# A hybrid decoder layer: the low half of the output stage's transposed operand moves from TensorE to a DMA transpose

## The chip, the cores and the metric

The kernel runs on one core of a Trainium2 chip. Its engines are TensorE (PE in the profile; PEld is its weight load), VectorE (DVE), ScalarE (ACT), GpSimd (POOL) and SyncE (SP), which issues the DMAs of this kernel. The metric is the device time of one execution in microseconds; less is better. A run's time is that of the whole execution, a profile's span reaches from the first to the last instruction.

## The reference

A decoder layer over 4096 positions of width 1024. Three groups of heads read one normalised input projection: a chunked gated MLP, a dilated attention in three dilations, and an attention into 256 memory tokens. Every branch is multiplied by its gate, the branches are laid side by side, and an output projection and the input are added:

```python
y = jnp.concatenate([y_g, y_a, y_m], axis=-1) @ w_out[l]
x = x + y
```

The change touches only this last product: `y` (4096 x 1024) times `w_out` (1024 x 1024), plus `x`.

## The kernel before

The kernel goes over the 32 tiles of 128 positions in several passes. Passes A and B project queries, keys, values and a gate, with the attention woven in; pass C (`pass_c`) does the memory attention and the gated MLP, and at its end begins the output stage. In between, results lie in DRAM: the three attention outputs (`o_d`), the gate (`ag_d`), the two other branches (`y_d`).

The output stage works tile by tile. `prep_y(n)` loads what it needs (tile `fo`, three parts, L742 and L743; `fsg`, L745; `fy`, L747 and L748; `fx`, the rows of x, L750), adds the three dilations (L751, L752), divides and gates (L754 to L759), finds each row's largest value (L762 to L765), and splits the scaled row into two f16 numbers: the high half on ACT (L767), the low half, what is left, on DVE (L768). Both are halves of one tile `hl` (name `fhl`), which has one buffer. TensorE transposes each half in eight 128x128 blocks into PSUM (L773, tile `fpt`), and ACT copies the result into `yT` (L774, name `fyT`, two buffers). `fo` and `fy` have two buffers each, `fsg` one.

The loop at the end calls `prep_y(n + 2)` and then does the product of tile n: `proj` (L222) multiplies high with high, high with low, and low with high, eight blocks each, so 24 matmuls of 512 columns and twice 24 of 256 columns, 72 in all (tile `fps`). `fin` scales and adds x (L977, L978), and the result is stored (L989).

The order of the instructions on each engine is not written out. A planner fixes it when the kernel is built, from modelled costs, with the order of the program as priority; at run time every engine and SP's queue of DMAs work strictly in that order. In the order that it found, the transposes of tile n + 2 stand between the 512-wide and the 256-wide matmuls of tile n.

Two earlier passes use a DMA transpose too: `qk_out` turns an `hl` tile of the same shape, 128 x 1024 in f16, into half of `stg` (L309), which ACT then copies (L312).

Of the kernel before, what the change touches and what calls it, by code (L numbers as in the profile page):

```python
# [9 lines left out]
F16 = mybir.dt.float16  # L10
# [8 lines left out]
P = 128  # L19
# [3 lines left out]
KT = D // P  # L23
# [11 lines left out]
def bcast(ap, n):  # L35
    s = list(ap.shape)
    return ap.unsqueeze(len(s)).broadcast_to(s + [n])
# [6 lines left out]
def shuffled(ap):  # L44

    return ap.rearrange("(j r) d -> r j d", r=R16)
# [25 lines left out]
def tile_hybrid_layer(ctx, tc, x, mem, norm_gain, w_in, gv_gain, wsT, gb, aqg, akg,  # L72
                      mem_gain, w_kv, mqg, mkg, w_out, out):
    nc = tc.nc
    V, S, G, TE, Q = nc.vector, nc.scalar, nc.gpsimd, nc.tensor, nc.sync
# [6 lines left out]
    def ps_tile(tag, shape, dt, name):  # L82
        return pp.tile(shape, dt, tag="po" if tag == "tr" else tag, name=name)
# [17 lines left out]
    idh = cp.tile([P, P], F16, name="idh")  # L101
# [249 lines left out]
    with tc.tile_pool(name="pA", bufs=2) as pA:  # L351
# [46 lines left out]
        for n in range(NT):  # L398
# [57 lines left out]
            if n == 12:  # L456
                wM, scM = got("wM")
                for j in range(2):
# [5 lines left out]
                    hl = pm.tile([P, 8, 2, HD], F16, name=f"mhl{j}", tag="hl", bufs=2)  # L464
# [274 lines left out]
    def prep_y(n):  # L739
        ot = pools[0].tile([P, 3, NH, 65], F32, name=f"fo{n}", tag="fo")  # L740
        for ci in range(2):
            Q.dma_start(ot[:, ci], o_d[ci][n * P:(n + 1) * P])  # L742
        Q.dma_start(ot[:, 2], o_d[2].rearrange("(r n j) h c -> n r j (h c)", r=R16, j=8)[n])  # L743
        sg = pools[0].tile([P, 512], F32, name=f"fsg{n}", tag="fsg", bufs=1)
        Q.dma_start(sg, shuffled(ag_d[n]))  # L745
        y = pools[0].tile([P, D], F32, name=f"fy{n}", tag="fy")
        Q.dma_start(y[:, 0:256], shuffled(y_d[n][:, 0:256]))  # L747
        Q.dma_start(y[:, 768:1024], shuffled(y_d[n][:, 256:512]))  # L748
        xr = pools[0].tile([P, D], F32, name=f"fx{n}", tag="fx", bufs=3)
        Q.dma_start(xr, shuffled(x[n * P:(n + 1) * P, :]))  # L750
        V.tensor_add(ot[:, 0], ot[:, 0], ot[:, 1])  # L751
        V.tensor_add(ot[:, 0], ot[:, 0], ot[:, 2])  # L752
        rd = pools[0].tile([P, NH], F32, name=f"frd{n}", tag="frd")
        V.reciprocal(rd, ot[:, 0, :, 64])  # L754
        yv = y[:, 256:768].rearrange("p (h c) -> p h c", c=HD)
        V.tensor_tensor(yv, ot[:, 0, :, 0:64], bcast(rd, HD), ALU.mult)
        for i in range(2):
            ys = y[:, 256 + i * 256:512 + i * 256]
            V.scalar_tensor_tensor(ys, ys, fag[:, i:i + 1], sg[:, i * 256:(i + 1) * 256],  # L759
                                   ALU.mult, ALU.mult)  # L760
        a = pools[0].tile([P, 8], F32, name=f"fa{n}", tag="fa", bufs=4)
        V.tensor_reduce(a[:, 0:1], y, AX.X, ALU.max, apply_absolute_value=True)  # L762
        V.tensor_scalar_max(a[:, 0:1], a[:, 0:1], 1e-30)
        V.reciprocal(a[:, 1:2], a[:, 0:1])
        V.tensor_scalar_mul(a[:, 1:2], a[:, 1:2], 2.0 ** 14)  # L765
        hl = pools[0].tile([P, 2, D], F16, name=f"fhl{n}", tag="fhl", bufs=1)
        S.activation(hl[:, 0, :], y, AF.Copy, scale=a[:, 1:2])  # L767
        V.scalar_tensor_tensor(hl[:, 1, :], y, a[:, 1:2], hl[:, 0, :], ALU.mult, ALU.subtract)  # L768
        yT = pools[0].tile([P, 2, KT, P], F16, name=f"fyT{n}", tag="fyT", bufs=2)
        for c in range(2):  # L770
            pt = ps_tile("po", [P, KT, P], F16, f"fpt{n}_{c}")
            for k in range(KT):
                TE.transpose(pt[:, k, :], hl[:, c, k * P:(k + 1) * P], idh)  # L773
            S.copy(yT[:, c], pt)  # L774
        yTs[n] = (yT, a, xr)

    pools, pool_cm = [], []
# [92 lines left out]
    def pass_c():  # L870
        xTs = {}
        for n in range(NT + LAG):
# [87 lines left out]
            if n == NT - 1 + SHIFT2:  # L960
                prep_y(0)
                prep_y(1)
# [7 lines left out]
    for n in range(NT):  # L970
        if n + 2 < NT:
            prep_y(n + 2)
        yT, a, xr = yTs.pop(n)
        res = pm.tile([P, D], F32, name=f"fr{n}", tag="stg", bufs=2)

        def fin(ps, c0, c, sc, k):
            V.tensor_scalar(a[:, k:k + 1], a[:, 0:1], sc[:, 0:1], 2.0 ** -28, ALU.mult, ALU.mult)  # L977
            V.scalar_tensor_tensor(res[:, c:c + 256], ps[:, c0:c0 + 256], a[:, k:k + 1],  # L978
                                   xr[:, c:c + 256], ALU.mult, ALU.add)

        ps = ps_tile("pj", [P, 512], F32, f"fps{n}_0")
        proj(ps, yT, wO0, 512)
        fin(ps, 0, 0, scO0[0], 2)
        fin(ps, 256, 256, scO0[1], 3)
        for i, (w, sc) in enumerate(ready["wO1"]):
            ps = ps_tile(("ps", "pa")[i], [P, 512], F32, f"fps{n}_{i + 1}")
            proj(ps, yT, w, 256)
            fin(ps, 0, 512 + 256 * i, sc, 4 + i)
        Q.dma_start(shuffled(out[n * P:(n + 1) * P, :]), res)  # L989
# [37 lines left out]
```

## Time and profile before

| | |
|---|---|
| time, median of three runs | 2130.55 us (2123.88 to 2132.16) |
| the profiled execution's own time | 2122.38 us |
| its span, first to last instruction | 2120.7 us |
| mean granted TensorE clock | 0.982 of 2.4 GHz |
| TensorE matmul busy | 1999.8 us, 94% |
| VectorE busy | 1467.6 us, 69% |
| ScalarE busy | 1204.4 us, 57% |
| GpSimd busy | 685.2 us, 32% |
| DMA, mean | 161 GB/s |
| output stage, first transpose to end | 1727.8 to 2120.7 us |

Busy shares are means over the whole span, and each stage has another limit; the output stage is the last 393 us of it. In the rows further down, an instruction has its start and its length in us, its engine, its line, what it writes and reads, and in brackets the engine's idle time before it with what ended that.

### The profile page before, as it was taken

The numbers are of one execution on the slowest core, as the hardware profiler recorded it, in microseconds if no ns is written. First come the engines' busy times: TensorE is split into PE (matmuls) and PEld (weight loads), VectorE is DVE, ScalarE is ACT, GpSimd is POOL, SyncE is SP. The second block draws the span as 40 slices with busy tenths as digits, with TensorE's granted clock in tenths as the row PEclk, the third lists the DMA queues.
The fourth block names the chain that finished last, engine by engine and source line by source line (L and its number), as shares of the span: only waits on it lengthen the run. The fifth ranks groups of instructions, "written<-read, shape, count | busy, mean of one in ns | idle before, by whom it ended". The sixth has DMA issues, their size and how long they took to land.

```text
span 2120.7 us, 45749 instructions
## 1 busy us (share of the span) xinstructions
PE 1999.8 (94%) x17025; PEld 1291.9 (61%) x17025; DVE 1467.6 (69%) x4332; ACT 1204.4 (57%) x2048; POOL 685.2 (32%) x632
## 2 busy tenths in 40 slices
PE   5999999988999998998999998999999989999999
PEld 4444444434466565665776766767757766767766
DVE  7665465466578686687787877868766676767762
ACT  6676676444478586684675765756757732222221
POOL 1212212121056264453554653535635620000000
PEclk9999999999999999999999999999999999999999
DMA  6777687585557868666447365474453367767662
GB/s 219 200 201 202 178 197 181 139 228 142 161 129 170 221 139 202 162 169 160 114 94 186 87 155 147 92 185 98 92 137 86 81 175 194 219 209 218 204 189 70
DMA packets 468959, 341.00 MB, mean 161 GB/s; under 512 B 294400, under 2 KB 404096, under 8 KB 466944
## 3 DMA queue, kind: packets, MB, share of 16 engines
q1 hardware_dynamic: 468736, 338.08, 62.1%
q8 instruction: 133, 2.18, 0.4%
q14 instruction: 90, 0.74, 0.1%
HBM read 198.52 MB, written 113.84 MB: 147 GB/s over the span
## 4 chain that ended last, share of the span: by engine, by line
PE 52%; DMA 6%; DVE 6%; issue 3%; ACT 3%; SPq 1%; POOL 1%; ACTq 0%; DVEq 0%; POOLq 0%
PE fps L222 15%; PE pc L222 13%; PE pag L222 4%; PE pqb L222 3%; PE s L588 3%; PE s L590 3%; PE pa L491 2%; PE o L615 1%; PE o L613 1%; PE o L611 1%; PE fpt L773 1%; DMA qn<-qnd 1%; DVE e L593 1%; DVE jk L498 1%; DMA qm<-q2t 1%
## 5 line engine op out<-in xcount | busy, mean ns | idle before, releaser
L545 POOL TENSOR_TENSOR pl<-e,ph 128x512 f16<-128x512 f32 (+1 forms) x384 | 412.0, 1085 | 342.3 <-ACT ph L544 246.9
L222 PE MATMUL pc<-wC,xTc 128*128 128x512 f16 (+1 forms) x2304 | 473.9, 346 | 1.9 <-ACT rw_c L259 1.2
L498 DVE CUSTOM_DVE_ANT_0 jk<-pa,mask 128x256 bf16<-128x256 f32 (+1 forms) x768 | 300.7, 391 | 86.1 <-PE pa L491 64.2
L222 PE MATMUL fps<-wO,fyT 128*128 128x256 f16 (+1 forms) x2304 | 341.7, 309 | 0.0
L595 ACT ACTIVATE e<-e,gas 128x512 f32<-128x512 f32 (+1 forms) x384 | 253.3, 674 | 129.1 <-DVE e L593 128.2
L222 PEld LDWEIGHTS <-xTc 128*128 128x128 f16 x2304 | 220.5, 99 | 149.7 <-issue 7.0
L222 PEld LDWEIGHTS <-fyT 128*128 128x128 f16 x2304 | 224.8, 98 | 103.5 <-issue 2.8
L593 DVE TENSOR_TENSOR e<-s,mask 128x512 f32<-128x512 f32 (+1 forms) x384 | 235.1, 627 | 54.2 <-PE s L590 43.1
L222 PEld LDWEIGHTS <-xTa 128*128 128x128 f16 x1608 | 158.3, 100 | 176.6 <-issue 12.2
L222 PEld LDWEIGHTS <-xTb 128*128 128x128 f16 x1536 | 150.0, 99 | 155.8 <-issue 17.2
L271 POOL TENSOR_TENSOR r_q<-r_q,mhalf 128x8 f32<-128x8 f32 x64 | 114.5, 1790 | 381.8 <-DVE r_q L269 359.7
L544 ACT CAST ph<-e 128x512 f16<-128x512 f32 (+1 forms) x384 | 212.3, 569 | 18.8 <-PE o L615 14.4
L222 PE MATMUL pqb<-wQ,xTb 128*128 128x512 f16 x768 | 191.5, 391 | 2.2 <-DVE sc_wC L179 1.8
L588 PE MATMUL s<-q,k 128*128 128x256 f16 (+1 forms) x768 | 179.3, 264 | 11.5 <-DMA q<-qkpd 4.6
L222 PE MATMUL pag<-wAG,xTb 128*128 128x512 f16 x768 | 186.8, 381 | 2.5 <-ACT rw_q L259 2.1
L222 PE MATMUL pv<-wV,xTa 128*128 128x512 f16 (+1 forms) x840 | 179.3, 370 | 5.4 <-DVE vt L287 4.7
L222 PE MATMUL pq<-wQ,xTa 128*128 128x512 f16 x768 | 173.7, 382 | 1.6 <-DVE wQ L174 1.2
L590 PE MATMUL s<-q,k 65*128 65x256 f16 (+1 forms) x768 | 170.9, 264 | 2.6 <-DMA q<-cm 2.6
L611 PE MATMUL o<-vr,ph 128*128 128x65 f16 x1368 | 169.3, 193 | 1.8 <-ACT ph L544 1.7
L491 PE MATMUL pa<-kp,qn 128*128 128x256 f16 (+1 forms) x768 | 137.8, 268 | 33.9 <-DVE mx L498 16.5
L613 PE MATMUL o<-vr,ph 128*128 128x64 f16 x1368 | 168.7, 194 | 0.0
L615 PE MATMUL o<-vr,pl 128*128 128x65 f16 x1368 | 158.0, 193 | 8.3 <-POOL pl L545 8.0
(282 smaller groups left out, 3363.9 us busy)
## 6 DMA issues: line engine op xcount, KB each, us to landing
vr<-vd SPq DMA_DIRECT2D x48, 520.0 KB
fo<-od SPq DMA_DIRECT2D x96, 260.0 KB
od<-ot SPq DMA_DIRECT2D x128, 130.0 KB
x_a<-in_x_dram SPq DMA_DIRECT2D x32, 512.0 KB
xTd<-xTa SPq DMA_DIRECT2D x32, 512.0 KB
xTb<-xTd SPq DMA_DIRECT2D x32, 512.0 KB
xTc<-xTd SPq DMA_DIRECT2D x32, 512.0 KB
fx<-in_x_dram SPq DMA_DIRECT2D x32, 512.0 KB
```

What stands on the lines that cost most here:

```text
L222: last = TE.matmul(ps[:, :n], xt[:, a, k, :], w[:, b, k, c:c + n], start=(k == 0 and a == 0 and b == 0), stop=(k == KT - 1 and a == 1))
L491: TE.matmul(pa[:, i, 256 - w:256], qn[:, q0:q0 + (P - 1) * d + 1:d], packed(kp, d, r, max(b - 1, 0), w), start=True, stop=True)
L498: V.tensor_tensor_reduce(jk[:, :w], pa[:, i, 256 - w:256], masks[d][:, 256 - w:256], 1.0, -3e38, ALU.add, ALU.max, mx[:, mc:mc + 1])
L544: S.copy(ph[:, :w], e[:, :w])
L545: G.tensor_sub(pl[:, :w], e[:, :w], ph[:, :w])
L588: TE.matmul(st[:, i, :n], k1[:, kk], packed(q1, d, r, b, n), start=True, stop=False)
L590: TE.matmul(st[:, i, :n], k2[:, kk], packed(q2, d, r, b, n), start=False, stop=True)
L593: V.tensor_tensor(e[:, :w], st.rearrange("p a q -> p (a q)")[:, :w], masks[d][:, :w], ALU.add)
L595: S.activation(e[:, :w], e[:, :w], AF.Exp, scale=asg[:, 2:3])
L611: TE.matmul(o[:, slot, 0:65], hi[:, c:c + 128], v[:, 0:65], start=(j == 0), stop=False)
L613: TE.matmul(o[:, slot, 0:64], hi[:, c:c + 128], v[:, 66:130], start=False, stop=False)
L615: TE.matmul(o[:, slot, 0:65], lo[:, c:c + 128], v[:, 0:65], start=False, stop=(j == len(terms) - 1))
```

## The change

In `prep_y`, the loop over the two halves goes. The low half of `hl` is transposed by one DMA transpose issued from SP's queue straight into `yT`; the high half is transposed by TensorE and copied by ACT as before.

```diff
         yT = pools[0].tile([P, 2, KT, P], F16, name=f"fyT{n}", tag="fyT", bufs=2)
-        for c in range(2):
-            pt = ps_tile("po", [P, KT, P], F16, f"fpt{n}_{c}")
-            for k in range(KT):
-                TE.transpose(pt[:, k, :], hl[:, c, k * P:(k + 1) * P], idh)
-            S.copy(yT[:, c], pt)
+        Q.dma_start_transpose(yT[:, 1], hl[:, 1, :])
+        pt = ps_tile("po", [P, KT, P], F16, f"fpt{n}")
+        for k in range(KT):
+            TE.transpose(pt[:, k, :], hl[:, 0, k * P:(k + 1) * P], idh)
+        S.copy(yT[:, 0], pt)
         yTs[n] = (yT, a, xr)
```

`Q` is SP's queue, `S` is ACT, `TE` is TensorE; the numbers of buffers stay as they are.

## Rows read from the trace of the kernel before

**Rows 1.** The page's first part: busy us, share of the span, instructions.
```profile
PE 1999.8 (94%) x17025; PEld 1291.9 (61%) x17025; DVE 1467.6 (69%) x4332; ACT 1204.4 (57%) x2048; POOL 685.2 (32%) x632
```

**Rows 2.** Windows of 40 us: start, end, length, busy by engine, granted clock, DMA share, GB/s.
```profile
1720.00:1760.00 40.00, 35.82 (x270) 23.51 (x271) 31.79 (x93) 11.22 (x15) 1.69 (x2) 0.96 0.68 180
...
1880.00:1920.00 40.00, 40.00 (x308) 27.27 (x306) 28.04 (x72) 11.09 (x12) 0.00 (x0) 1.00 0.74 224
```

**Rows 3.** Chain of waits in order of time, 1700 us on: start, length, what.
```profile
1794.61 0.89 PE fpt L773 x16
...
1816.91 0.89 PE fpt L773 x16
1817.80 10.42 PE fps L222 x72
...
2054.49 0.89 PE fpt L773 x16
...
2089.32 26.09 PE fps L222 x192
```

**Rows 4.** Groups by line, 1760 to 2080: count, busy, mean ns, idle before and releaser.
```profile
L774 ACT COPY fyT<-fpt 128x1024 f16<-128x1024 f16 x56 | 54.0, 1014 | 94.7 <-PE fps L222 87.8 <-PE fpt L773 6.9
L978 DVE SCALAR_TENSOR_TENSOR fr<-fps,fa,fx 128x256 f32<-128x256 f32 x111 | 50.6, 477 | 21.9 <-PE fps L222 21.8
...
L767 ACT ACTIVATE fhl<-fy,fa 128x1024 f16<-128x1024 f32 x29 | 33.3, 1149 | 132.3 <-PE fpt L773 96.9 <-issue 27.1 <-DVE fo L752 8.3
...
L751 DVE TENSOR_TENSOR fo<-fo 128x520 f32<-128x520 f32 x26 | 18.2, 700 | 39.3 <-DMA fo<-od 39.3
L752 DVE TENSOR_TENSOR fo<-fo 128x520 f32<-128x520 f32 x26 | 18.2, 700 | 22.9 <-DMA fo<-od 22.8
```

**Rows 5.** Timeline of SP's queue over one tile: start, length, line, DMA issued.
```profile
1912.07 0.51 SPq L747 DMA_DIRECT2D fy<-yd  x1
...
1913.32 1.01 SPq L742 DMA_DIRECT2D fo<-od  x2
...
1915.00 0.59 SPq L743 DMA_DIRECT2D fo<-od  x1
...
1916.32 0.59 SPq L750 DMA_DIRECT2D fx<-in_x_dram  x1
1922.67 0.51 SPq L747 DMA_DIRECT2D fy<-yd  x1
```

**Rows 6.** Timeline of DVE in the same tile.
```profile
1916.97 0.70 DVE L751 TENSOR_TENSOR fo<-fo 128x520 f32<-128x520 f32 x1 [1.38 <-DMA fo<-od]
...
1919.74 0.70 DVE L752 TENSOR_TENSOR fo<-fo 128x520 f32<-128x520 f32 x1 [1.26 <-DMA fo<-od]
...
1921.37 1.27 DVE L768 SCALAR_TENSOR_TENSOR fhl<-fy,fa,fhl 128x1024 f16<-128x1024 f32 x1
```

**Rows 7.** Timeline of ACT in the same tile.
```profile
1913.58 1.93 ACT L774 COPY fyT<-fpt 128x1024 f16<-128x1024 f16 x2 [3.43 <-PE fps L222]
1919.71 1.15 ACT L767 ACTIVATE fhl<-fy,fa 128x1024 f16<-128x1024 f32 x1 [4.20 <-PE fpt L773]
```

**Rows 8.** Timeline of DVE: the splits of tiles 7 and 28, two of 32.
```profile
1811.42 1.28 DVE L768 SCALAR_TENSOR_TENSOR fhl<-fy,fa,fhl 128x1024 f16<-128x1024 f32 x1 [0.56 <-ACT fhl L767]
...
2045.34 1.28 DVE L768 SCALAR_TENSOR_TENSOR fhl<-fy,fa,fhl 128x1024 f16<-128x1024 f32 x1 [0.47 <-ACT fhl L767]
```

**Rows 9.** Timelines of SP and ACT: two of 64 earlier DMA transposes, with their readers.
```profile
344.52 1.26 SPq L309 DMA_TRANSPOSE stgA<-hl  x1
...
348.97 2.04 ACT L312 COPY stpA<-stgA 128x1024 f16<-128x1024 f16 x1 [3.25 <-DMA stgA<-hl]
...
695.25 5.58 SPq L309 DMA_TRANSPOSE stgB<-hl  x1
...
707.75 2.04 ACT L312 COPY stpB<-stgB 128x1024 f16<-128x1024 f16 x1 [6.32 <-DMA stgB<-hl]
```

**Rows 10.** Window over one earlier DMA transpose whose data move alone.
```profile
535.30:536.45 1.15, 1.15 (x7) 0.53 (x6) 0.00 (x0) 0.00 (x0) 0.00 (x0) 1.00 1.01 228
```

## The prediction

> **What bounds the kernel now.** Only the output stage is touched, so the page's busy shares [rows 1] say little: they average over stages with different limits. I first read the windows of 40 us. In the middle of the output stage TensorE is busy for all 40.00 us at full granted clock, DVE for 28, ACT for 11, and the DMA engines for 0.74 of their time; the window at the stage's start is less even [rows 2]. The chain of waits then shows one tile's period: 0.89 us for 16 transposes and 10.42 us for 72 matmuls, 11.31 us together, with TensorE next to itself the whole way [rows 3]. So TensorE bounds this stage, and what it drops is gained, as long as nothing else needs more than the new period.
>
> The groups by line show how near the others are. DVE waits for DMA loads of `fo` (L751 39.3 us, L752 22.8 us) and little for TensorE (L978 21.8 us) [rows 4]. The timelines show why. SP's `fy` loads (L747) go out as soon as DVE's split (L768, the low half of `hl`) of the tile two earlier has freed the buffer: the split of 1921.37 ends at 1922.64, the issue starts at 1922.67. A round before, `fy` was issued at 1912.07 and the `fo` loads of a later tile behind it, until 1915.59; DVE's next add (L751) waits for these until 1916.97 and the second (L752) until 1919.74, and only behind that in DVE's order stands the split of 1921.37 [rows 5, 6]. This is a ring of DVE, SP and DMA with its own length. The splits of tiles 7 and 28 (counted from 0) start at 1811.42 and 2045.34 [rows 8]: 233.92 us over 21 rounds, 11.14 us a round. TensorE's transposes come 4.2 us after the split of tile 7 is done (1816.91 against 1812.70) and 7.9 us after that of tile 28 (2054.49 against 2046.62) [rows 3, 8]. The ring is thus faster than TensorE by less than 0.2 us a tile. That is the point of this case: two limits lie side by side.
>
> **What the change removes.** Per tile eight of 16 transposes: half of 0.89 us, 0.445 us of TensorE, on the path while TensorE is the bound. From tile 5 (1794.61 [rows 3]) on the chain is transposes and matmuls alone, so 27 tiles: 27 x 0.445 = 12.0 us at most. It also removes one ACT copy per tile, 1.01 us [rows 4]; ACT is busy for 11 us in 40 [rows 2] and the copy waits for TensorE anyway, so this is worth nothing. The PSUM buffer that it saves is nothing that anyone is seen to wait for.
>
> **What it adds.** One DMA transpose per tile on SP, 128x1024 f16 from SBUF to SBUF. The stages before hold the same shape (`stg <- hl`, L309), so the trace has its price. SP is taken for 1.26 us [rows 9]. Alone, its data fill the 16 DMA engines for about 1.15 us (share 1.01, 228 GB/s) [rows 10]. From issue to the reader's start it took 4.45 us in a quiet case (344.52 to 348.97), and 12.5 us in a crowded one, where the issue alone held SP for 5.58 us (695.25 to 707.75) [rows 9]. Over 32 tiles this is 40 us of SP and 37 us of all DMA engines, and what counts is where it falls.
>
> DMA throughput has room: 0.74 x 11.31 = 8.4 us a tile [rows 2] plus 1.15 is 9.5 us of a period of 10.87. Three waits are new.
>
> First, `yT` has two buffers, so the transpose can't be issued before the 256-wide matmuls of the tile two earlier have read the old one; the ACT copy shows that moment, 1913.58 [rows 7]. Behind it on SP stand the `fo` loads (1913.32 and on), `fsg`, the store of the result and `fx` [rows 5].
>
> Second, `hl` has one buffer, so ACT's first write of the next tile (L767) now waits for the landing as well as for TensorE, the cause of 96.9 us of its idle time in this stretch [rows 4]. From 1913.4, 4.45 us lead to 1917.9, before 1919.71 where L767 starts today [rows 7]: free. 12.5 us lead to 1925.9, and then 1.15 us on ACT and 1.27 us on DVE put the end of the split at 1928.3 instead of 1922.64, a round longer by 5.7 us. I take the short price, since the transfer would be issued early in a burst, not behind a full queue as at 695.25; the long one stays for the range.
>
> Third, the place on SP. Between the `fy` and `fo` issues (just before 1913.32) the transpose moves the `fo` loads, and with them L751, L752 and the split, by its 1.26 us. Behind the last `fo` issue (1915.59) it moves none of them; its data then come after those for which L752 waits until 1919.74, and land about 1.15 us later, at 1920.9; with 1.15 and 1.27 us the split ends at 1923.3, 0.7 us later than today. I take 1.26 us, because the buffer falls free just where the first place is, and keep 0.7 us as the low end. A gain of the ring is excluded: nothing is taken out of it.
>
> On a rule that speaks against this: eight 128x128 blocks took 0.445 us on TensorE and about 1.15 us of data and 4.45 us in all as one DMA transpose [rows 3, 9, 10]. The Trainium skill, "VectorE: DVE Perf Modes", section "The three transpose paths", gives 390 ns for a block on TensorE and 1309 ns for one by DMA, and the rules at its end prefer TensorE where the result may go to PSUM. At 1309 ns for each of eight blocks a transpose would take an estimated 10.5 us, and by the second wait above the split would end near 1926.3, 3.7 us late. The trace doesn't bear out that price for a multi-block transfer: the order of the two paths agrees, the size doesn't.
>
> **The sum.** The ring goes from 11.14 to 12.40 us. From tile 7 to tile 28, the last split that a `fo` load hangs on, 21 rounds grow by 26.5 us. The 7.9 us by which TensorE is behind today are used up first: 18.6 us are left at the transposes of tile 28. Tiles 4 to 6 run before that in the uneven first part, where DVE and DMA already set the pace: 3 x 1.26 = 3.8 us more. From tile 28 on there are no `fo` loads, and TensorE runs at its own, shorter pace: 4 x 0.445 = 1.8 us back. The last 26 us of matmuls [rows 3] don't change. Sum: 18.6 + 3.8 - 1.8 = 20.6 us slower. The profiled execution took 2122.38 us (span 2120.7); the median of the three runs is 2130.55, 8 us higher, so I add the difference to the median: 2151 us.
>
> **The rivals.**
> 1. Hidden: the transpose finds SP's idle time (1916.91 to 1922.67 [rows 5]) or the `fo` loads are issued before it, and the landing stays within the slack. TensorE then stays the bound at 10.87 us. For it speaks that both ring and DMA have some air; against it that 11.14 is already above 10.87, so that over 21 tiles 21 x 0.27 = 5.7 us are needed where 4.2 us of lead are there. Gain 12.0 - 1.5 = 10.5 us, up to 12: 2119.
> 2. Half hidden: the place behind the `fo` loads, 0.7 us a round: 14.7 - 7.9 + 2.1 - 1.8 = 7 us slower; with less in the first tiles about zero. 2130 to 2138.
> 3. Blocked, far slower: the transpose stands ahead of the `fo` loads in SP's order while its buffer falls free late. Once TensorE's lead is used up, transposes start when L767 is done, and the 0.445 us and 48 matmuls of 256 (half of 10.42 us) that free the buffer follow: 5.65 us after L767, which ends 1.78 us before the split does (1920.86 against 1922.64), so 3.9 us after the split. The `fo` loads then start 3.9 + 1.26 us after the split instead of 1.28, and the round is 11.14 + 3.9 = 15.0 us: 21 x 3.9 - 7.9 + 3.8 - 1.8 = 76 us slower, 2207. It decides as soon as the ring is longer than TensorE's period. For it: SP issues strictly in order. Against it: the planner that fixes the order may put the loads first. A landing of 12.5 us comes to the same size.
>
> **How the numbers follow.** Forecast 0.47, hidden 0.25, half hidden 0.10, blocked 0.18. The forecast alone runs from 8 to 36 us slower (0.7 to 2 us a round). The range takes in the hidden case and the centre of the blocked one: 2118 to 2208. About 0.5%, 10.7 us, can be told from no change. Hidden lies on that line: 0.12 faster, 0.13 same. Half hidden is same, 0.10, and so is the small end of the forecast, 0.08. The rest, 0.39 + 0.18 = 0.57, is slower.
>
> **What would show it.** In the chain after, the steady alternation of `fpt` and `fps` breaks, and pieces of DVE and `fo` loads come in. TensorE shows idle time ahead of `fpt` that ends with L767 or L768, summing to some 20 us. Splits of tiles 7 and 28 lie about 260 us apart. L751 and L752 wait longer for `fo`, and L767 for the landing rather than for TensorE only where that is later. If the chain shows x8 transposes at 0.445 us and x72 matmuls with no gap, rival 1 holds and my ring was no limit. If SP waits long at the transpose itself, rival 3 holds. What would make it wrong at all: an order of instructions on DVE or SP in which the loads no longer stand between two splits.

## The result, and the profile after

| | before | after |
|---|---|---|
| time, median of four runs each | 2127.22 us (2123.71 to 2132.16) | 2154.97 us (2151.38 to 2158.1) |
| ratio after/before, 95% interval | | 1.0111 (1.0089 to 1.0134) |
| profiled execution, time and span | 2122.38, 2120.7 us | 2153.48, 2151.6 us |
| first transpose of the output stage | 1727.8 us | 1740.0 us |
| output stage, from there to the end | 392.9 us | 411.6 us |

The change makes the kernel 1.1% slower, some 24 us by the ratio and 19 to 28.5 us by its interval; the two medians are 27.75 us apart. Of the 31 us between the two profiled executions, 18.7 lie in the output stage, and the stage is what the rest of this text explains. It grew by 4.8%, while its mean granted clock (1760 to 2080 us) was 0.99 before and 0.98 after, so the clock by itself doesn't make the difference. The other 12.2 us lie ahead of it, where both kernels have the same instructions in the same order; they first differ at the last tile of pass C. They are taken up at the end.

The page's first part of after, with the columns of [rows 1]: TensorE's total is the same to 0.2 us although 256 transposes are gone, so a total tells nothing here.

```profile
PE 2000.0 (93%) x16769; PEld 1280.8 (60%) x16769; DVE 1465.9 (68%) x4332; ACT 1174.5 (55%) x2016; POOL 684.0 (32%) x632
```

The windows of after in the middle of the stage, with the columns of [rows 2]: TensorE was busy for all 40.00 us and now has gaps of 5 us. The DMA share rose from 0.74 to about 0.9. ACT fell from 11.09 us to 6.4, and nobody is the faster for it.

```profile
1880.00:1920.00 40.00, 34.73 (x242) 23.18 (x241) 23.65 (x57) 6.43 (x7) 0.00 (x0) 0.96 0.91 201
1960.00:2000.00 40.00, 35.01 (x255) 23.43 (x252) 25.43 (x61) 6.78 (x7) 0.00 (x0) 1.00 0.88 204
```

Groups by line of after, 1760 to 2110 us (27 adds where [rows 4] have 26), which answer to [rows 4]. The high half (L767) waited for TensorE's transposes before, now for the landing of the DMA transpose. The first `fo` add (L751) waits 96.4 us where it waited 39.3, the second (L752) 10.3 where it waited 22.9. TensorE's transposes (L773) wait 32.4 us for L767.

```profile
L767 ACT ACTIVATE fhl<-fy,fa 128x1024 f16<-128x1024 f32 x28 | 32.1, 1148 | 139.6 <-DMA fyT<-fhl 123.2 <-DVE fr L978 11.8 <-DVE fa L762 4.6
...
L751 DVE TENSOR_TENSOR fo<-fo 128x520 f32<-128x520 f32 x27 | 18.9, 700 | 96.4 <-DMA fo<-od 96.4
L752 DVE TENSOR_TENSOR fo<-fo 128x520 f32<-128x520 f32 x27 | 18.9, 700 | 10.3 <-DMA fo<-od 9.9
L773 PE MATMUL fpt<-idh,fhl 128*128 128x128 f16 x230 | 18.7, 225 | 32.4 <-ACT fhl L767 32.4
```

The chain of waits of after, one round, in order of time. Where [rows 3] had TensorE next to itself, there now stands the ring: issue of `fo` on SP, its landing, the second add, the search for the row maximum (L762), the split (L768), and the next issue. At four places between the splits of tiles 7 and 28 the chain goes through the landing of the DMA transpose instead; the longest of these is the row by itself.

```profile
1991.73 0.30 SPq L742
...
1992.77 5.28 DMA fo<-od
...
1998.15 0.71 DVE fo L752
...
1999.47 1.23 DVE fa L762
...
2001.62 1.20 DVE fhl L768
```

```profile
1853.79 7.14 DMA fyT<-fhl
```

The timeline of DVE in the same round, with the columns of [rows 6]:

```profile
1988.93 1.28 DVE L768 SCALAR_TENSOR_TENSOR fhl<-fy,fa,fhl 128x1024 f16<-128x1024 f32 x1
...
1996.98 0.70 DVE L751 TENSOR_TENSOR fo<-fo 128x520 f32<-128x520 f32 x1 [4.08 <-DMA fo<-od]
1998.15 0.70 DVE L752 TENSOR_TENSOR fo<-fo 128x520 f32<-128x520 f32 x1 [0.47 <-DMA fo<-od]
...
1999.47 1.22 DVE L762 TENSOR_REDUCE fa<-fy 128x1 f32<-128x1024 f32 x1
...
2001.35 0.14 DVE L765 TENSOR_SCALAR fa<-fa 128x1 f32<-128x1 f32 x1
...
2001.53 1.27 DVE L768 SCALAR_TENSOR_TENSOR fhl<-fy,fa,fhl 128x1024 f16<-128x1024 f32 x1
```

And two rows of DVE's timeline before, from the tile of [rows 6]:

```profile
1914.38 1.22 DVE L762 TENSOR_REDUCE fa<-fy 128x1 f32<-128x1024 f32 x1
...
1918.20 0.15 DVE L765 TENSOR_SCALAR fa<-fa 128x1 f32<-128x1 f32 x1
```

Here is what the diff doesn't show. Before, DVE did the search (L762 to L765) between the split and the second add, while it waited for `fo` anyway. After, the planner has put the search of the next tile between the second add and the split, inside the ring. From the start of the second add to the end of the split it was 2.91 us (median of 21 rounds), and is 4.66 us.

The timelines of SP and ACT in the same round, with the columns of [rows 5] and [rows 7]:

```profile
1990.23 0.52 SPq L747 DMA_DIRECT2D fy<-yd  x1
...
1991.48 1.24 SPq L742 DMA_DIRECT2D fo<-od  x2
1992.77 0.53 SPq L743 DMA_DIRECT2D fo<-od  x1
1993.40 0.54 SPq L745 DMA_DIRECT2D fsg<-agd  x1
1994.04 1.27 SPq L770 DMA_TRANSPOSE fyT<-fhl  x1
```

```profile
1993.13 1.01 ACT L774 COPY fyT<-fpt 128x1024 f16<-128x1024 f16 x1 [4.75 <-PE fps L222]
1999.70 1.15 ACT L767 ACTIVATE fhl<-fy,fa 128x1024 f16<-128x1024 f32 x1 [5.55 <-DMA fyT<-fhl]
```

The transpose (L770) stands behind the `fo` loads and behind `fsg`. SP's order moved here too: before, `fsg` stood ahead of the last `fo` load (L743, 1915.00 in [rows 5]), and now it stands behind all three.

```profile
1914.42 0.53 SPq L745 DMA_DIRECT2D fsg<-agd  x1
```

The first `fo` issue comes 1.28 us after the split's end in both kernels (medians), so the transpose holds up no issue of a `fo` load. Its own data land late: 1994.04 to 1999.70 is 5.66 us. From the start of L767 it takes 1.15 us on ACT and 1.27 us on DVE to the end of the split. DVE's own ring ends this split at 2002.80; L767 ends at 2000.85, 0.68 us before the split starts. So there are two rings of nearly one length: through `fo` and the search, and through the transpose's landing.

The splits of tiles 7 and 28 of after, as in [rows 8], and TensorE's transposes of tile 28:

```profile
1824.27 1.28 DVE L768 SCALAR_TENSOR_TENSOR fhl<-fy,fa,fhl 128x1024 f16<-128x1024 f32 x1
...
2088.76 1.28 DVE L768 SCALAR_TENSOR_TENSOR fhl<-fy,fa,fhl 128x1024 f16<-128x1024 f32 x1
```

```profile
2087.95 0.62 PE L773 MATMUL fpt<-idh,fhl 128*128 128x128 f16 x8 [2.17 <-ACT fhl L767]
```

264.49 us over 21 rounds, 12.59 us each, where it was 11.14.

### The profile page after: what moved, and what is told of

Its sections match the earlier page's. It is cut to its first block, busy times and chain, and to the rows that moved or that the text cites. A ratio compares the mean times of both kernels' runs of the same rounds, so it can differ in the third digit from the quotient of the medians.

```text
span 2151.6 us, 45268 instructions
## 1 busy us (share of the span) xinstructions
PE 2000.0 (93%) x16769; PEld 1280.8 (60%) x16769; DVE 1465.9 (68%) x4332; ACT 1174.5 (55%) x2016; POOL 684.0 (32%) x632
## 4 chain that ended last, share of the span: by engine, by line
PE 30%; DMA 10%; DVE 10%; issue 3%; SPq 2%; ACT 1%; POOL 0%; DVEq 0%; ACTq 0%; POOLq 0%
PE pc L222 14%; DMA fo<-od 5%; PE fps L222 4%; PE s L588 2%; PE s L590 2%; DMA fyT<-fhl 2%; PE pa L491 2%; DVE fr L978 1%; DVE fhl L768 1%; DVE fa L762 1%; DVE e L593 1%; DMA qn<-qnd 1%; PE o L615 1%; PE o L613 1%; PE o L611 1%
```

## The experiments

"Order held" below means that DVE's search is kept where it stands in the kernel before. "Round" is the mean from the split of tile 7 to that of tile 28, "stage" the time from the first output transpose to the end in the profile. Each ratio is against the kernel before on the same chip.

| kernel | time, us | ratio (95%) | round | stage |
|---|---|---|---|---|
| low half not transposed | 2150.79 | 1.0105 (1.0072 to 1.0138) | 12.89 | 414.2 |
| same, order held | 2110.66 | 0.9925 (0.9902 to 0.9948) | 10.63 | 372.5 |
| the change, order held | 2148.48 | 1.0088 (1.0045 to 1.0131) | 12.44 | 404.2 |
| before, search moved into the ring | 2172.77 | 1.0203 (1.0165 to 1.0241) | 13.43 | 438.6 |
| the change, two `hl`, order held | 2141.87 | 1.0033 (1.0016 to 1.0051) | 11.94 | 400.6 |
| the change, split tiles, order held | 2125.80 | 0.9949 (0.9934 to 0.9963) | 10.80 | 382.3 |
| the change, two `hl` | 2176.09 | 1.0179 (1.0157 to 1.0200) | 13.29 | 427.9 |
| before plus a DMA transpose | 2222.46 | 1.0404 (1.0379 to 1.0429) | 15.68 | 480.8 |
| the change, split tiles | 2174.31 | 1.0203 (1.0185 to 1.0222) | 13.54 | 431.1 |
| before, split tiles, order held | 2131.08 | 0.9997 (0.9986 to 1.0009) | 11.09 | 386.9 |

SP's order, and on DVE the place of the scalings (L978), were left to the planner, so "order held" is not the whole order of the kernel before: in each of these kernels `fsg` stands behind all `fo` loads, as in the change, and between the second add and the split there are one or no scalings, where the kernel before has two.

The first four ask whether order or transfer made the change slow.

**Low half not transposed at all.** The DMA transpose is taken out, and the product reads the high half twice.

```diff
-        Q.dma_start_transpose(yT[:, 1], hl[:, 1, :])
-                last = TE.matmul(ps[:, :n], xt[:, a, k, :], w[:, b, k, c:c + n],
+                last = TE.matmul(ps[:, :n], xt[:, min(a, xt.shape[1] - 1), k, :], w[:, b, k, c:c + n],
```

> The low half is not transposed at all, by neither path, and the product reads the high half twice; the split on DVE stays. The planner is left free. Theory of the prediction (the DMA transpose on SP and the DMA queue lengthens the ring): without it TensorE's gain is left, 6 to 12 us faster than before. Theory found in the trace after (the planner, with TensorE's work shortened, put the search for each row's largest value, L762 to L765, between the second add of fo and the split): the search is in the ring here too, and L767 of ACT as well; a round is about 7.9 us from a split to the second add, plus 0.7 + 0.45 + 0.2 + 2.05 + 1.15 + 1.28 us, 13.7 us in all, so 30 to 50 us slower than before.

Measured: 1.0105, some 22 us slower. This is the direction of the second theory, but less than its 30 to 50 us. With less work than either kernel it is as slow as the change. In this order the split stands behind its own tile's search and its own high half, all in the ring. The window and the groups of this kernel:

```profile
1880.00:1920.00 40.00, 33.92 (x248) 22.67 (x245) 24.85 (x65) 6.14 (x6) 0.00 (x0) 1.00 0.63 183
```

```profile
L768 DVE SCALAR_TENSOR_TENSOR fhl<-fy,fa,fhl 128x1024 f16<-128x1024 f32 x20 | 25.7, 1284 | 23.4 <-ACT fhl L767 23.4
```

TensorE is idle for 6 of 40 us with the DMA engines at 0.63, and DVE waits 23.4 us for ACT's L767 over 20 splits. No transfer is needed to make this loss: taking eight transposes from TensorE is enough for the planner to choose another order.

**The same with the order held.** The adds of a tile are placed around the search of the tile three earlier.

```diff
-        V.tensor_add(ot[:, 0], ot[:, 0], ot[:, 1])
-        V.tensor_add(ot[:, 0], ot[:, 0], ot[:, 2])
+        with tc.issue_after(found[n - 3][0].ins) if n > 2 else nullcontext():
+            V.tensor_add(ot[:, 0], ot[:, 0], ot[:, 1])
+        with tc.issue_after(found[n - 3][1].ins) if n > 2 else nullcontext():
+            V.tensor_add(ot[:, 0], ot[:, 0], ot[:, 2])
```

> As e1, with DVE held to the order of before: the search of a tile ahead of the adds of fo. Theory of the trace after: 5 to 12 us faster than before, as the ring is back at 11.1 us or less and TensorE's period is 10.87 us. Theory of the prediction: the same as e1, 6 to 12 us faster, and equal to e1 within 3 us.

Measured: 0.9925, some 16 us faster than before where 5 to 12 were expected, and 40 us less than the run above on the same work. Its window and its chain:

```profile
1880.00:1920.00 40.00, 40.00 (x296) 27.78 (x295) 29.54 (x72) 7.63 (x7) 0.00 (x0) 1.00 0.75 220
```

```profile
1953.56 0.45 PE fpt L775 x8
1954.00 10.42 PE fps L222 x72
```

TensorE is never idle and needs 10.87 us a tile. The whole gain of the removed transposes is there once the order stays, and more than the 12.0 us that the prediction counted for it; the round is 10.63 us: 11.14 was not the least that the ring can do.

**The change with the order held.** The division (L756) is made to stand ahead of the search of the tile before.

```diff
-        V.tensor_tensor(yv, ot[:, 0, :, 0:64], bcast(rd, HD), ALU.mult)
+        gated = V.tensor_tensor(yv, ot[:, 0, :, 0:64], bcast(rd, HD), ALU.mult)
+        if founds:
+            tc.add_manual_dep(founds[-1].ins, gated.ins.name, ...)
```

> The change whole, with DVE held to the order of before (the search behind the split and the division). If the order of DVE is the cause alone: within 5 us of the kernel before. If the second ring of the trace after is as long (issue of the transpose behind the fo and fsg loads 4.5 us after the split, 5.5 us to the landing, 1.15 us ACT, 1.28 us DVE: 12.4 us): 10 to 22 us slower than before. If SP and DMA alone are the cause, as predicted: 20 to 28 us slower, no better than the change.

Measured: 1.0088, and a round of 12.44 us. So the order alone doesn't pay either. By time alone the second and the third case of the expectation can't be told apart (the interval runs from 10 to 28 us); the group and the chain speak for the second. Its group and its chain (the added lines move L767 to L771):

```profile
L771 ACT ACTIVATE fhl<-fy,fa 128x1024 f16<-128x1024 f32 x21 | 24.1, 1147 | 107.7 <-DMA fyT<-fhl 81.9 <-DVE fr L983 25.9
```

```profile
1959.93 5.02 DMA fyT<-fhl
...
1965.10 1.16 ACT fhl L771
...
1966.29 1.29 DVE fhl L772
```

The other ring has taken over: the transpose's issue 4.07 us after the split (median), its landing, the next high half, the next split, with nothing of `fo` between.

**Before, with the search moved into the ring.** The split is held behind the next tile's search.

```diff
+        if splits:
+            tc.add_manual_dep(splits[-1].ins, found.ins.name, ...)
```

> The kernel before, all on TensorE, with the split of a tile held behind the search of the next tile, as in the order after. Theory of the trace after: the ring grows from 11.1 to 12.3 to 12.9 us, 21 rounds less the 7.9 us by which TensorE is behind: 15 to 30 us slower than before. Theory of the prediction (the DMA transpose is the cause): within 4 us of before.

Measured: 1.0203, with no DMA transpose in it. Its chain is that of after:

```profile
1962.29 4.82 DMA fo<-od
...
1968.22 0.61 DVE fo L752
...
1969.45 1.23 DVE fa L762
...
1971.47 1.19 DVE fhl L771
```

The direction is plain, the size isn't: 43 us where 15 to 30 were expected, and a round of 13.43 us, longer than in the change. SP's order moved too (`fsg` now stands ahead of two of the `fo` loads), and the landing on the chain lets go the first add, with one of the scalings of the result between it and the second. Which of these makes the rest wasn't tried.

The next ones ask what frees the second ring.

**Two `hl` buffers, order held.** The adds as above, and:

```diff
-        hl = pools[0].tile([P, 2, D], F16, name=f"fhl{n}", tag="fhl", bufs=1)
+        hl = pools[0].tile([P, 2, D], F16, name=f"fhl{n}", tag="fhl", bufs=2)
```

> The change with DVE in the order of before and hl with two buffers, so that ACT's write of the next high half no longer waits for the landing of the DMA transpose just issued. If the landing of the transpose is what held e3 at 12.4 us a round: the round falls to 10.9 to 11.3 us, and the kernel is 3 to 12 us faster than the kernel before (2113 to 2122 for 2125). If the transpose's place on SP or its share of the DMA engines is the cost: still 10 us or more slower than before, with a round near 12.4 us.

Measured: 1.0033, better than one buffer but no gain; the expectation missed. The waits of ACT and of SP (total, times, longest, us):

```profile
ACT fhl L770 <- DVE frd L756: 128.5, 13, 10.8
ACT fhl L770 <- DMA fyT<-fhl: 77.6, 8, 10.6
```

```profile
SPq L773 <- PE fps L222: 14.9, 18, 1.2
```

The second `hl` would let the high half run ahead, but the destination `yT` still has two buffers. The transpose now goes out one tile later, behind the next split, and waits there on SP for TensorE to have read the old `yT`, so the high half of the tile after waits for it again. (The first row puts 13 of these waits down to a reciprocal on DVE that had ended 0.5 to 0.9 us before L770 started; L770 started 5.2 to 6.7 us after the transpose's issue in these rounds as in the others, so they are read as waits for the landing too, which is an inference.) A buffer at the source alone moves the wait to the destination.

**Split tiles, order held.** High and low get tiles of their own, the low half with two buffers at the source and three at the destination, so that only the low half waits for a landing. The adds as above, and:

```diff
+        hh = pools[0].tile([P, D], F16, name=f"fhh{n}", tag="fhh", bufs=1)
+        hw = pools[0].tile([P, D], F16, name=f"fhw{n}", tag="fhw", bufs=2)
...
+        yh = pools[0].tile([P, KT, P], F16, name=f"fyh{n}", tag="fyh", bufs=2)
+        yw = pools[0].tile([P, KT, P], F16, name=f"fyw{n}", tag="fyw", bufs=3)
+        Q.dma_start_transpose(yw, hw)
```

> As e5, with the halves in tiles of their own: low half of hl two buffers, high half one, low half of yT three buffers, high half two, so that the transpose also need not wait for the matmuls of the tile two earlier. If that wait costs nothing once hl is freed: equal to e5 within 4 us. If it does: 4 us or more faster than e5, down to the 2110 of e2.

Measured: 0.9949, 2125.80 against 2136.85 us: faster than the kernel before, by 11 us. Its window, its chain and the group of the first add (the added lines make L751 and L752 into L752 and L754):

```profile
1880.00:1920.00 40.00, 40.00 (x290) 26.86 (x289) 27.61 (x71) 7.71 (x8) 0.00 (x0) 1.00 1.02 244
```

```profile
1956.17 0.45 PE fpt L778 x8
1956.62 10.42 PE fps L222 x72
```

```profile
L752 DVE TENSOR_TENSOR fo<-fo 128x520 f32<-128x520 f32 x25 | 17.5, 698 | 43.7 <-DMA fo<-od 43.6
```

TensorE is the bound again from 1840 us on, at 0.45 and 10.42 us a tile, with the DMA engines at a share of 1.02; between 1800 and 1840 us it still had 5 us of gaps. Against the kernel without any transpose of the low half, the first add waits 43.6 us for `fo` instead of 6.0, and the ratio is 0.9949 instead of 0.9925. The two intervals overlap, so these runs show no cost of the transfer itself beyond the noise; their difference would be 0.24%, some 5 us, when nothing waits for the landing.

**The control: split tiles in the kernel before, order held.** Same buffers, same order, but both halves by TensorE.

```diff
-        Q.dma_start_transpose(yw, hw)
+        for c, (src, dst) in enumerate(((hh, yh), (hw, yw))):
```

> The control for e6: the same buffers and the same order held on DVE, but both halves transposed by TensorE and copied by ACT, no DMA transpose. If e6's gain is TensorE's shorter period: within 4 us of the kernel before, TensorE busy throughout at 11.31 us a tile. If the buffers or the order brought it: as fast as e6, 8 to 14 us faster than before.

Measured: 0.9997, no difference. So neither buffers nor order make the kernel before faster, and the gain of the run above belongs to the DMA transpose. (The profiled stages of the two, 382.3 and 386.9 us, are only 4.6 us apart while the ratios differ by 0.48%, some 10 us; the timed runs weigh more than one profile.)

**Buffers without the order.** Two `hl`, and split tiles, each with the planner left free; the edits are those shown, without the part on the adds.

> The change with two buffers for hl and the planner left free. If the order of DVE that the planner finds is enough by itself to cost what the change cost: about as e1, 20 to 30 us slower than before, although the landing is no longer waited for. If the landing alone is the cause: 3 to 12 us faster than before.

> The buffers of e6, the planner left free: it puts the search of a tile and the wait for ACT between the second add and the split, as in e1. If the order of DVE costs by itself once the landing is out of the way: 20 to 35 us slower than before, a round near 13 us. If the landing was the real cause and the order only follows it: within 5 us of e6, 5 to 15 us faster than before.

Measured: 1.0179 and 1.0203, worse than the change itself: some 38 and 43 us slower than before, where 20 to 30 and 20 to 35 were expected. The planner again put the search into the ring, here that of the same tile, with the high half behind it. In the split tiles DVE waits for it right ahead of the split:

```profile
1903.60 1.28 DVE L769 SCALAR_TENSOR_TENSOR fhw<-fy,fa,fhh 128x1024 f16<-128x1024 f32 x1 [1.22 <-ACT fhh L768]
```

Four kernels thus stand as a table of two causes. Planner's order, landing waited for (the change): 1.0111. Order held, landing waited for: 1.0088. Planner's order, landing free: 1.0203. Order held, landing free: 0.9949. To mend the order alone brings 0.2%, which the intervals don't tell from nothing; to free the landing alone is worse than nothing; to mend both brings 1.6%. The table isn't a clean one: the planner's order of the third kernel is another than that of the change, and the order of the second is held by another edit than that of the fourth.

**The kernel before plus a DMA transpose.** The low half is also transposed by DMA, into a tile that nobody reads.

```diff
+        yd = pools[0].tile([P, KT, P], F16, name=f"fyd{n}", tag="fyd", bufs=2)
+        Q.dma_start_transpose(yd, hl[:, 1, :])
```

> The kernel before, all 16 transposes on TensorE, plus the same DMA transpose of the low half into a tile of two buffers that nobody reads. It costs SP, DMA and the wait of hl, without TensorE's gain. If the landing held against the one buffer of hl is what costs: a round of 12 us or more, 10 to 30 us slower than before. If the transpose is cheap where it stands: within 5 us of before.

Measured: 1.0404, a round of 15.68 us, far outside both cases of the expectation. It was to show the transfer's own cost, and it doesn't: the planner changed SP's order. Part of one round of SP's timeline:

```profile
1911.48 1.26 SPq L771 DMA_TRANSPOSE fyd<-fhl  x1
1912.84 0.54 SPq L747 DMA_DIRECT2D fy<-yd  x1
...
1917.01 1.42 SPq L742 DMA_DIRECT2D fo<-od  x1
1918.48 0.54 SPq L743 DMA_DIRECT2D fo<-od  x1
```

The transpose, the `fy` loads and (left out here) the store and `fx` stand ahead of the last `fo` loads. What this run prices is above all a bad place on SP, not the transfer. (The granted clock was lower too, 0.94 from 1800 to 2060 us where the split tiles with the order held had 0.99.)

## Why the prediction was right, and where its steps were wrong

The forecast was 2151 us, 20.6 us slower; measured were 2154.97 and 18.7 us in the stage. Direction and size were right, and so was the frame: two limits side by side, TensorE and a ring of DVE, SP and DMA, and the ring growing past TensorE. By its terms:

| term of the sum | predicted | measured |
|---|---|---|
| first tiles, up to the split of tile 7 | +3.8 | +0.7 |
| 21 rounds of the ring | +26.5 (12.40 a round) | +30.6 (12.59) |
| lead of the ring over TensorE, used up | -7.9 | -10.0 |
| tail from tile 28 | -1.8 | -2.6 |
| sum | +20.6 | +18.7 |

The first term compares the split of tile 7 with the first transpose (1811.42 - 1727.8 = 83.6 us, 1824.27 - 1740.0 = 84.3). The second is 264.49 against 233.92 us. The last is from TensorE's transposes of tile 28 to the end: 66.2 and 63.6 us.

**The round was right in size and wrong in its reason.** The prediction's third step put the transpose on SP between the `fy` and `fo` issues and took +1.26 us from that. It stands behind `fo` and `fsg`, and the `fo` issue isn't later at all. The second add even starts a little earlier after the split (7.86 us against 8.06, means of the 21 rounds). What grew is the way from that add to the end of the split: 4.73 against 3.08 us, +1.65. Together, 1.65 - 0.20 = 1.45 us, this is the whole growth of the round. The near agreement of 1.26 and 1.45 is chance. As what would make it wrong at all, the prediction had named an order on DVE or SP in which the loads no longer stand between two splits. The loads still stand there; what moved is the search, an order that it neither named nor priced. Why the planner chose this order wasn't tried; shown is that it also leaves the old order when the transposes are merely dropped.

**The second wait was priced as free and isn't.** The step took 4.45 us from an issue at 1913.4, about 1.4 us after the split's end. The issue came 3.84 us after it, and the high half, which the landing lets go, started 5.56 us after the issue (medians of the 21 rounds; 3.83 and 5.66 us in the round shown). With the order held this wait alone makes a round of 12.44 us. So the change had two faults of nearly equal size, and one hid the other. In these rounds the reader of the DMA transpose of all eight blocks started 4.0 to 7.2 us after the issue. The estimated 10.5 us, which the prediction worked out from the Trainium skill ("VectorE: DVE Perf Modes", "The three transpose paths"), isn't borne out by these rows. The same page's preference for TensorE ("Rules for kernel authors") holds for the change as made and not for the split tiles with the order held: there TensorE is the bound, and the DMA transpose gains 0.5%.

**"A gain of the ring is excluded" was wrong.** The 11.14 us a round was read as the ring's own length. It was an upper bound: L767 spent 96.9 us waiting for TensorE in that stretch [rows 4], so TensorE set part of the pace. Without the low half's transpose and with the split tiles, order held, the rounds are 10.63 and 10.80 us, though part of this may be the other changes of order in these two kernels (`fsg` behind all `fo` loads, no scaling between the second add and the split). This was the main argument against the hidden case, and it was weak.

**The lead** was sized too small because the split no longer releases TensorE: the high half needs L767 only, and the transposes of tile 28 start 2.1 us before the split's end (2087.95 against 2090.04) instead of 7.9 us after it. **The first tiles** came out near by chance. The ring did grow there, by more than was charged: from the split of tile 4 to that of tile 7 it took 37.9 us where it took 27.5. But the split of tile 4 came 9.9 us sooner after the first transposes (46.4 us against 56.2), where the planner's order is another too; nothing was tried on this. **The tail** was right in kind: without `fo` loads TensorE runs at 10.87 us a tile, as these rows of the chain of after show. The last matmuls, which the prediction took as unchanged, are 1.2 us shorter: 181 instead of the 192 of [rows 3], since the last transposes stand 11 matmuls later in TensorE's order.

```profile
2110.30 10.42 PE fps L222 x72
2120.72 0.45 PE fpt L773 x8
2121.17 24.89 PE fps L222 x181
```

**What was removed** was priced right: 0.445 us of TensorE a tile, at most 12.0 us, and nothing for the ACT copy. The split tiles with the order held gain 11 us.

**The rivals.** Hidden, at 10.5 to 12 us faster, is what the split tiles reach with the order held: its mechanism is real, but needs buffers and an order that the change doesn't have. Half hidden had the right place on SP, behind the `fo` loads, and the right path, through the landing and the high half to the split, but put it at 0.7 us a round; with the order held the runs show 1.30 (12.44 against 11.14). Blocked, at 15.0 us a round with the transpose ahead of `fo` on SP, is close to the round of the kernel before with the added transpose (15.68), but not by its mechanism: there the transpose went out 0.03 us after the split's end and waited for no buffer, and the store and other loads stood ahead of `fo` as well.

## What to carry to other kernels

Where a planner sets the order, an edit that shortens one engine's work can move the instructions of another, so compare the order of the two kernels on each engine before pricing the edit's own parts, and hold the old order in one experiment. A transfer that takes over an engine's copy brings its landing into every buffer it touches: give source and destination a buffer more, and split a tile whose halves now have different readers (the three were tried together here, and paid only with the order held). A round's length read from a loop that another engine also paces is an upper bound, not the loop's own length.

## What the runs showed of the hardware that was not expected

With the split tiles the DMA engines stood at a share of 1.02 and 244 GB/s in the window shown, and TensorE was busy throughout it; the first add waited for its loads more (43.6 against 6.0 us), and the order left room for that. A DMA transpose whose data move alone in 1.15 us [rows 10] took 4.0 to 7.2 us (median 5.56) from issue to its reader behind the `fo` loads, 4.45 in the quiet case [rows 9], and 2.8 to 4.1 us in tiles 28 to 30 of after, when no `fo` loads are left.

The part ahead of the output stage varies more than the effects under study. Over the profiles of twelve kernels, taken on several chips, whose instructions are the same there (but for the last 20 us in two of them), the first output transpose started between 1727.8 us (before) and 1749.8; after, at 1740.0, lies in the middle. The mean granted clock up to 1700 us was 0.98 before and 0.97 after. So the 12.2 us by which the two profiles differ there are no effect of the change that any run shows. How much of the 27.75 us between the medians goes beyond the stage's 18.7 stays open.
